# Latent attention with queries on the partitions of the score tile and all keys along its free axis

## The chip, the core and the metric

The kernel runs on one core of a Trainium2 chip. The metric is the device time of one execution in microseconds (us). In the core, TensorE multiplies matrices and writes the results to PSUM, of which the kernel's pools take eight banks of 128 partitions x 512 fp32 numbers; VectorE does elementwise work and reductions along the free axis; ScalarE evaluates functions (exponentials among them) and makes copies; GpSimd and SyncE here issue DMA transfers. Every engine works through its own list of instructions in order and waits for semaphores of the others.

## What is computed

The reference is a two-layer network over 1024 latent tokens and 256 context tokens of width 1024. Layer 0 mixes tokens by multi-head latent attention, layer 1 by long convolutions (computed through block transforms on TensorE). The change is in the attention of layer 0, whose core in the reference is this (the context tokens' keys are set behind the latent tokens' keys, 1280 in all; `ctx_out` plays no part in the output):

```python
def scores(qn_, qr_, kn_, kr_):
    s = jnp.einsum('bqhd,bkhd->bhqk', qn_, kn_) + jnp.einsum('bqhr,bkr->bhqk', qr_, kr_)
    return s.astype(jnp.float32) * scale

def attend(blk):
    qn_b, qr_b = blk
    s = jnp.concatenate([scores(qn_b, qr_b, kn, kr), scores(qn_b, qr_b, knc, krc)], axis=-1)
    p = jax.nn.softmax(s, axis=-1).astype(v.dtype)
    return (jnp.einsum('bhqk,bkhd->bqhd', p[..., :L], v)
            + jnp.einsum('bhqk,bkhd->bqhd', p[..., L:], vc))
...
y = (o * jax.nn.silu(gate)) @ w_out
```

There are 8 heads. A head has 128 plain dimensions and shares 64 rotary dimensions of the key with all heads; values have 128 dimensions. Queries come from a compressed vector of 384, keys and values from one of 256.

## The kernel before

Nearly every product is done with split operands: a float32 matrix is taken apart into a rounded part (hi) and a rest (lo), both of type float32r, and a product is the sum of three matmuls, hi*hi + hi*lo + lo*hi. `mm3` (L117) issues them at L119, L120 and L121, and `split` (L95) makes the parts: ScalarE casts to hi at L96 and VectorE subtracts at L97. All these matmuls, casts and subtractions carry those lines, whatever they are for, so they are told apart by the names of their tiles.

Layer 0's input part leaves the compressed vectors `ckv` (keys and values, 1280 tokens) and `cq` (queries) in SBUF, the rotary keys as `krh` (hi, twice, on the two halves of the partitions) and `krl` (lo, and a 65th row of ones). `attention` (L651 to L850) goes through four pairs of heads (`pr`), two heads of a pair (`j`) and two halves of the queries (`sl`): 16 units of 512 queries of one head.

Ahead of a unit, `ahead` (L746) makes what it needs, through a pool of two PSUM banks "pj": `keys` (1280 keys of one head), `rope` (rotary parts of the queries, for both heads of the pair), `queries`, and then `row_max` (L724 to L739). The exponential needs the maximum of each query's scores, and in the unit's own score tiles the queries lie along the free axis, where a maximum over keys would go across partitions. So `row_max` computes the scores a second time the other way round, queries on the partitions, from the hi parts alone (one matmul at L731 and one at L732 for every 512 keys, in two banks "apx" of their own), takes maxima along the free axis (L733, L735), turns them into a row (L738) and puts that row, negated, into row 64 of the tile `r2` (L739). Together with the row of ones in `krl` it subtracts the maximum within the score matmul at L795.

`attend` (L773) then takes the ten tiles of 128 keys. Each has a score tile S of 128 keys x 512 queries, five matmuls (three of `mm3`, L794 and L795), in one of three banks; ScalarE exponentiates it (L797) into `p`; `split` makes its two parts; VectorE adds `p` to a running sum `acc` (L804); and two tiles later `weigh` multiplies the parts by the values of that tile (`value`, L680) into the bank O. Since keys lie on the partitions of `p`, it is the operand that this product needs as it stands. At the end of a unit the sums over keys are taken on TensorE (L821, a column of ones against `acc`), turned into reciprocals (L823), spread over all partitions (L828), and multiplied in together with the gate, a tile loaded from DRAM (L816, L829); the result goes to DRAM.

The loop at L833 interleaves the tiles of one unit with the tail of the one before it and with two steps of `ahead` for the next. In the last unit `out_first` (L873), the output projection of the first half of the tokens, takes the place of `ahead`. Within these bounds a planner sets the order of the instructions of each engine when the kernel is built, and so TensorE's list mixes matmuls of these pieces. PSUM holds two banks "pj", one O, three S and two "apx": all eight.

Layer 1 matters here for one thing: it turns 128x128 tiles on TensorE (L1033, L1168), with the same call that the change uses.

Of the kernel before, what the change touches and what calls it, by code (L numbers as in the profile page):

```python
# [11 lines left out]
F32 = mybir.dt.float32  # L12
# [7 lines left out]
P = 128  # L20
# [26 lines left out]
def run(gen):  # L47
    """The value that a generator returns."""
    while True:
        try:  # L50
            next(gen)
        except StopIteration as e:
            return e.value


class Net:
# [42 lines left out]
    def feed(self, tiles, bufs=3, side=None):  # L99
        """The weights [128, K * 128] of the coming projections, in their order."""  # L100
# [4 lines left out]
    def weights(self):  # L105
        """The next piece of the weights, the one after it being loaded as well."""
# [26 lines left out]
    def ada(self, layer, part, page, bank, width=1024, queue=None):  # L133
        """part 0: shift and scale, part 1: gate."""
# [66 lines left out]
    def ring(self, two, page, ze, zo, same):  # L201
        """Residues of 8-tile sequences ze (mod x^1024-1), zo (mod x^1024+1) in the 8 blocks."""
# [17 lines left out]
        B = [page().rearrange("p (s j c) -> p s j c", s=2, j=2) for _ in range(2)]  # [+-, j]  # L220
# [3 lines left out]
        t = page().rearrange("p (r s c) -> p r s c", r=2, s=2)  # [re/im, +-]  # L224
# [26 lines left out]
    def forward(self, two, bank, mats, i, b):  # L251
        """Spectrum of block i, [128, (re | im)] in one bank."""
# [92 lines left out]
    def rms(self, xs, n, bank, sqtile):  # L345
        """1/rms of n <= 512 tokens as columns [128, n / 128]."""
# [30 lines left out]
    def spread(self, r, nt, bank):  # L377
        """Columns [128, nt] as a row of nt*128 tokens on every partition."""
# [6 lines left out]
    def modulate(self, x, R, gs, sh, hi, lo):  # L385
        """x is overwritten by x*gs*R; hi + lo = that + shift."""
# [5 lines left out]
    def project(self, srcs, bank):  # L392
        """One M-tile: the next weights against each (hi tiles, lo tiles) of srcs; a bank for each."""
# [15 lines left out]
    def project_first(self, srcs, bank):  # L409
        """The same in the order of srcs; yields before the second of them."""  # L410
# [11 lines left out]
    def layer0_in(self):  # L422
# [13 lines left out]
        self.kr_d = [self.dram.tile([65, NK], F32, name=f"kr_d{r}") for r in range(2)]  # L436
# [39 lines left out]
        def hilo_out(t, n, dsts):  # L476
            """The two parts of t[:n] to DRAM, t being overwritten."""
# [19 lines left out]
        def context():  # L497
            # context: keys and values only
# [19 lines left out]
            hilo_out(ts[2], 64, [d[0:64, new] for d in self.kr_d])  # L518
            yield from normed(ts[:2], "kvg", self.ckv_d, new)
            one = page()  # L520
            v.memset(one[64:65, :], 1.0)
            for o in range(0, NK, LC):
                nc.sync.dma_start(out=self.kr_d[1][64:65, o : o + LC], in_=one[64:65, :LC])

        def latent_kv():
# [10 lines left out]
            for h, sl in enumerate(halves):  # L536
# [6 lines left out]
                hilo_out(t, 64, [d[0:64, sl] for d in self.kr_d])  # L543
            yield

        def latent_q():
# [8 lines left out]
            for h, sl in enumerate(halves):  # L555
                for _ in normed([t[h] for t in ts], "qg", self.att[3], sl, True):
                    next(more, None)
                    yield
# [49 lines left out]
    def attention_loads(self, side, raws):  # L608
# [3 lines left out]
        krh = ap.tile([P, NK], F32R, name="krh")  # L612
        krl = ap.tile([65, NK], F32R, name="krl")
# [5 lines left out]
        self.att = ckv, krh, krl, cq, cos, sin  # L619
# [31 lines left out]
    def attention(self):  # L651
        nc, a = self.nc, self.a
# [5 lines left out]
        ckv, krh, krl, cq, cos, sin = self.att  # L658
        self.og_d = self.dram.tile([HEADS, P, L], F32, name="og_d")
        identr = tp.tile([P, P], F32R, name="identr", bufs=1)  # L660
        act.copy(out=identr, in_=self.ident)
        pick = tp.tile([P, 4, P], F32, name="pick", bufs=1)
        v.memset(pick, 0.0)
        for t in range(4):
# [738 lines left out]
```

## Time and profile before

| | |
|---|---|
| time, median of 3 runs | 1750.57 us (1749.73 to 1758.41) |
| profiled execution: span from the first to the last instruction | 1753.2 us |
| granted TensorE clock, mean over the span | 0.995 |
| attention, from its first key projection to its last products | about 440 to 970 us |

The span is that of one execution under the profiler; the time of an execution also counts what lies around its first and last instruction, and for the profiled one no time is listed beside the span. The two agree within 0.2%.

How the profile is read: PE is a matmul on TensorE, PEld the load of its stationary operand, which overlaps matmuls; DVE is VectorE, ACT ScalarE, POOL GpSimd, SP SyncE. A row names the line of the kernel, the engine and operation, the tiles written and read (out<-in), shapes and types, and the number of instructions (x). Matmuls are pipelined: each has a duration longer than the distance between the starts of two neighbours. "Idle before" is the idle time of an engine right before the instructions of a row, with what ended it (<-). A small matmul of plain fp32 operands shows as two instructions.

### The profile page before, as it was taken

How to read it: one execution, taken by the hardware profiler on the slowest of the kernel's cores; microseconds unless marked ns; L12 is line 12 of the kernel's file. 1: busy time of each engine (PE TensorE's matmuls, PEld its weight loads, DVE VectorE, ACT ScalarE, POOL GpSimd, SP SyncE). 2: the span in 40 equal slices, each digit the busy share in tenths (PEclk: the TensorE clock that was granted, in tenths of full speed). 3: DMA queues.
4: the chain of work that ended last, by engine and by line, in shares of the span. 5: the costliest groups of instructions: out<-in, count | busy, mean ns of one | idle time of the engine just before them, and what ended most of it. 6: DMA issues, size and time to landing. Idle time of an engine off the chain costs nothing.

```text
span 1753.2 us, 23341 instructions
## 1 busy us (share of the span) xinstructions
PE 1687.9 (96%) x8368; PEld 1310.8 (75%) x8368; DVE 1408.3 (80%) x2528; ACT 759.3 (43%) x1315; POOL 15.1 (1%) x43
## 2 busy tenths in 40 slices
PE   7999999799999999999999999999999999999996
PEld 2367666687788888888877766888888888887874
DVE  4786978796687877887877455999999999999956
ACT  4533444435455555555555344433433343343313
POOL 1000000000000000000000010000000000000000
PEclk9999999999999999999999999999999999999999
DMA  9766666436101001010022772232332333234545
GB/s 308 249 186 193 193 199 204 138 93 194 36 27 43 19 29 40 19 32 25 19 67 79 245 249 87 84 101 88 106 114 81 104 87 111 91 118 128 188 149 209
DMA packets 139033, 207.23 MB, mean 118 GB/s; under 512 B 13386, under 2 KB 67361, under 8 KB 138788
## 3 DMA queue, kind: packets, MB, share of 16 engines
q1 hardware_dynamic: 135780, 195.05, 35.6%
q0 software_dynamic: 3136, 10.69, 1.9%
q8 instruction: 66, 1.08, 0.3%
q14 instruction: 51, 0.42, 0.1%
HBM read 149.97 MB, written 53.61 MB: 116 GB/s over the span
## 4 chain that ended last, share of the span: by engine, by line
PE 81%; DMA 9%; DVE 6%; ACT 2%; issue 1%; SPq 1%; DVEq 0%; ACTq 0%
PE pj L119 12%; PE pj L121 12%; PE pj L120 12%; PE apx L731 2%; PE S L119 2%; PE S L795 2%; PE S L120 2%; PE S L794 2%; PE S L121 2%; PE apx L732 2%; PE O L121 2%; PE O L120 2%; PE O L119 2%; PE fu L119 2%; DMA dec<-in_dec 2%; PE fy L119 2%
## 5 line engine op out<-in xcount | busy, mean ns | idle before, releaser
L96 ACT CAST w<-wr 128x512 fp32r<-128x512 f32 (+1 forms) x154 | 93.7, 609 | 276.0 <-PE pj L120 150.3
L119 PE MATMUL pj<-a,w 128*128 128x512 f32 x512 | 203.2, 397 | 1.7 <-ACT a L389 1.7
L120 PE MATMUL pj<-a,w 128*128 128x512 f32 x512 | 203.3, 397 | 0.0
L121 PE MATMUL pj<-a,w 128*128 128x512 f32 x512 | 203.1, 398 | 0.0
L797 ACT ACTIVATE p<-S 128x512 f32<-128x512 f32 x160 | 95.7, 598 | 167.6 <-PE S L795 160.7
L97 DVE TENSOR_TENSOR w<-wr,w 128x512 fp32r<-128x512 f32 (+1 forms) x154 | 102.0, 670 | 63.4 <-ACT w L96 63.0
L804 DVE TENSOR_TENSOR acc<-acc,p 128x512 f32<-128x512 f32 x144 | 99.1, 688 | 29.0 <-ACT p L797 28.6
L97 DVE TENSOR_TENSOR p<-p 128x512 fp32r<-128x512 f32 x160 | 109.7, 685 | 8.9 <-ACT p L96 8.6
L96 ACT CAST bh<-raw 128x512 fp32r<-128x512 f32 x128 | 77.1, 620 | 88.2 <-DVE raw L1043 70.3
L119 PEld LDWEIGHTS pj<-a,w 128*128 128x128 f32 x512 | 96.4, 188 | 22.9 <-ACT a L389 2.4
L120 PEld LDWEIGHTS pj<-a,w 128*128 128x128 f32 x512 | 96.5, 188 | 21.4 <-issue 1.7
L121 PEld LDWEIGHTS pj<-a,w 128*128 128x128 f32 x512 | 96.6, 189 | 18.5 <-DVE w L97 0.3
L733 DVE TENSOR_REDUCE cm<-apx 128x1 f32<-128x512 f32 (+1 forms) x192 | 108.3, 594 | 2.2 <-PE apx L732 1.5
L96 ACT CAST p<-p 128x512 fp32r<-128x512 f32 x160 | 99.4, 621 | 5.0
L121 PE MATMUL pj<-pg,w 128*128 128x512 f32 (+1 forms) x248 | 95.7, 387 | 4.2 <-DVE w L97 4.2
L119 PE MATMUL pj<-pg,w 128*128 128x512 f32 (+1 forms) x248 | 95.7, 387 | 0.6 <-ACT pg L389 0.5
L120 PE MATMUL pj<-pg,w 128*128 128x512 f32 (+1 forms) x248 | 96.3, 388 | 0.0
L97 DVE TENSOR_TENSOR bl<-raw,bh 128x512 fp32r<-128x512 f32 x128 | 84.5, 684 | 9.1 <-ACT bh L96 8.8
L119 PE MATMUL u<-bh,fm 128*128 128x256 f32 (+1 forms) x200 | 66.6, 334 | 11.1 <-ACT bh L96 10.7
L731 PE MATMUL apx<-kn,qn 128*128 128x512 f32 (+1 forms) x192 | 69.9, 369 | 2.9 <-DVE cm L733 2.8
L305 DVE TENSOR_TENSOR kk<-ph,dec 128x512 f32<-128x512 f32 x64 | 42.6, 684 | 32.9 <-DMA dec<-in_dec 20.0
L119 PE MATMUL fy<-bh,dm 128*128 128x256 f32 (+1 forms) x200 | 64.1, 320 | 2.4 <-ACT bh L96 2.4
(297 smaller groups left out, 4396.8 us busy)
## 6 DMA issues: line engine op xcount, KB each, us to landing
aw<-in_adaw SPq DMA_DIRECT2D x32, 512.0 KB, 5.0
kd<-ko SPq DMA_DIRECT2D x128, 128.0 KB, 2.0
wr<-in_hw SPq DMA_DIRECT2D x64, 256.0 KB, 2.6
kt<-kd SPq DMA_DIRECT2D x56, 256.0 KB, 2.7
wr<-in_w SPq DMA_DIRECT2D x34, 256.0 KB, 3.5
dec<-in_dec SPq DMA_DIRECT2D x64, 128.0 KB, 2.5
pg<-in_adaw SPq DMA_DIRECT2D x32, 256.0 KB, 6.1
wr<-in_wo SPq DMA_DIRECT2D x32, 256.0 KB, 3.2
```

Source lines behind the costliest of these rows:

```text
L96: self.nc.scalar.copy(out=hi, in_=raw)
L97: self.nc.vector.tensor_tensor(out=lo, in0=raw, in1=hi, op=ALU.subtract)
L119: mm(out, lhsT=w[0], rhs=x[0], start=start, stop=False)
L120: mm(out, lhsT=w[0], rhs=x[1], start=False, stop=False)
L121: mm(out, lhsT=w[1], rhs=x[0], start=False, stop=stop)
L305: nc.vector.tensor_tensor(out=kk, in0=ps, in1=dec.broadcast_to([P, 2, 2, P]), op=ALU.mult)
L731: mm(b[:, :w], lhsT=qn[0][:, c], rhs=kn[0][:, o : o + w], start=True, stop=False)
L732: mm(b[:, :w], lhsT=r1[:, c], rhs=krh[:, o : o + w], start=False, stop=True)
L733: v.tensor_reduce(out=cm[:, t, i : i + 1], in_=b[:, :w], axis=AX.X, op=ALU.max)
L794: mm(S, lhsT=krh[:, c], rhs=r1, start=False, stop=False)
L797: act.activation(out=p, in_=S, func=AF.Exp, scale=ASCALE)
L804: v.tensor_tensor(out=acc, in0=acc, in1=p, op=ALU.add)
```

## The change

The score tile is set the other way round. A unit is now 256 queries of one head, 32 units in all, each with two row blocks of 128 queries. `scores` computes a row block against all 1280 keys, 128 queries on the partitions and the keys along the free axis, in two and a half PSUM banks, with the same five products (the lo part of the rotary keys now lies in `kr[1]`, without a row of ones). VectorE reduces the whole row block to its maxima, negated, and ScalarE exponentiates it with that column as bias and gives the sums over the row as well. The factor of the softmax is moved into the queries.

Now the queries lie on the partitions of `p`, and the product with the values wants the keys there. So `turn` transposes two key tiles of both row blocks on TensorE (four transposes of 128x128) into a bank and splits them from there, and `weigh` multiplies them by the values, 256 queries at a time. `norm` turns the reciprocals of the sums in the same way and multiplies the gate by them, and O is multiplied by that once. `row_max`, `acc`, the sums on TensorE and the constant tiles `identr` and `pick` are gone, with the row of ones and the five small transfers that wrote it.

PSUM is split anew: five banks for two row blocks of scores (the third is shared by them), one O, and two banks "m" for everything else. The loop issues, for each of five steps of a unit, one `turn`, one or two pieces of the scores of the next units, one `weigh` of the step before, and up to three matmuls' worth (on a running account) of `ahead`. Weights of the next pair are loaded as soon as the keys and queries of this pair are issued. `out_first` begins with the last but one unit and opens its PSUM banks only when its heads are loaded.

The core of the diff, with `attention`'s removed lines left out where they are printed above:

```diff
-        bank = lambda: ps.tile([P, 512], F32, tag="pj", name="pj")
-        px = self.open("psX", 2, space=PSUM)
+        bank = lambda: ps.tile([P, 512], F32, tag="m", name="m")
+        S = self.open("psX", 1, space=PSUM).tile([P, 2 * NK], F32, name="S")
         tp = self.open("attt", 2)
...
+        ssegs = [ksegs, [(256, 512), (768, 512), (0, 256)]]
...
-            self.split(b, qn[0], qn[1])
+            act.activation(out=qn[0], in_=b, func=AF.Copy, scale=ASCALE)
+            v.scalar_tensor_tensor(out=qn[1], in0=b, scalar=ASCALE, in1=qn[0], op0=ALU.mult, op1=ALU.subtract)
...
-        def row_max(kn, qn, r1, r2):
-            cm = tp.tile([P, 4, 3], F32, tag="cm", name="cm")
...
-        units = [(pr, j, sl) for pr in range(HEADS // 2) for j in range(2) for sl in halves]
+        units = [(pr, j, h, q) for pr in range(HEADS // 2) for j in range(2) for h in range(2) for q in range(2)]
...
+            nxt = self.kvw, *self.qw
             for pr in range(HEADS // 2):
+                wc, wq, wr = nxt
                 vals[pr] = (wc, [])
                 rr = {}
                 for j in range(2):
+                    while at["unit"] // 4 < 2 * pr + j - 1:
+                        yield None
+                    kn = [tp.tile([P, NK], F32R, tag=f"kn{r}", name="kn") for r in range(2)]
+                    yield from keys(wc, j, kn)
+                    if j == 1 and pr + 1 < HEADS // 2:
+                        wc = self.load_kv_weights(pr + 1)
+                    for h, sl in enumerate(halves):
+                        while at["unit"] // 2 < 4 * pr + 2 * j + h - 2:
+                            yield None
                         if j == 0:
+                            rr[h] = yield from rope(wr, sl)
                         qn = queries(wq, j, sl)
+                        ready[pr, j, h] = (kn, qn, rr[h][j])
+                        yield 9
+                if pr + 1 < HEADS // 2:
+                    nxt = wc, *self.load_q_weights(pr + 1)
...
+        credit = 0
+        def advance(n):
+            nonlocal credit
+            credit = min(credit + n, n)
+            while credit > 0:
+                cost = next(bg, None)
+                if cost is None:
+                    break
+                credit -= cost
+        def need_values(pr, n):
+            while len(vals[pr][1]) < n:
+                vals[pr][1].append(value(vals[pr][0], len(vals[pr][1])))
+        live = {}
+        def scores(u, s):
+            pr, j, h, q = units[u]
+            at["unit"] = max(at["unit"], u)
+            while (pr, j, h) not in ready:
+                next(bg)
+            kn, qn, r1 = ready[pr, j, h]
+            if s == 0:
+                stat = [tp.tile([P, 2], F32, tag=f"s{i}", name="stat", bufs=4) for i in range(3)]
+                gate = tp.tile([P, 256], F32, tag="gt", name="gt", bufs=3)
+                o = 512 * h + 256 * q
+                nc.sync.dma_start(out=gate, in_=self.gate_d[2 * pr + j, :, o : o + 256])
+                live[u] = {"p": [], "stat": stat, "gate": gate}
+            me = live[u]
+            nm, sm, _ = me["stat"]
+            c = slice(256 * q + P * s, 256 * q + P * s + P)
+            base = NK * s
+            for o, w in ssegs[s]:
+                b, ks = S[:, base + o : base + o + w], slice(o, o + w)
+                mm(b, lhsT=qn[0][:, c], rhs=kn[0][:, ks], start=True, stop=False)
+                mm(b, lhsT=qn[0][:, c], rhs=kn[1][:, ks], start=False, stop=False)
+                mm(b, lhsT=qn[1][:, c], rhs=kn[0][:, ks], start=False, stop=False)
+                mm(b, lhsT=r1[:, c], rhs=kr[0][:, ks], start=False, stop=False)
+                mm(b, lhsT=r1[:, c], rhs=kr[1][:, ks], start=False, stop=True)
+                if (o, w) != ssegs[s][-1]:
+                    yield
+            row = S[:, base : base + NK]
+            v.tensor_reduce(out=nm[:, s : s + 1], in_=row, axis=AX.X, op=ALU.max, negate=True)
+            p = tp.tile([P, NK], F32, tag="p", name="p", bufs=4)
+            act.activation(out=p, in_=row, func=AF.Exp, bias=nm[:, s : s + 1], accum_out=sm[:, s : s + 1])
+            me["p"].append(p)
+        def turn(u, k):
+            me = live[u]
+            b = bank()
+            for i in range(2):
+                t = 2 * k + i
+                for s in range(2):
+                    o = 256 * i + P * s
+                    nc.tensor.transpose(out=b[:, o : o + P], in_=me["p"][s][:, P * t : P * t + P], identity=self.ident)
+            me[k] = [tp.tile([P, 512], F32R, tag=f"p{r}", name="pe", bufs=4) for r in range(2)]
+            self.split(b, *me[k])
+        def norm(u):
+            me = live[u]
+            _, sm, r = me["stat"]
+            v.reciprocal(out=r, in_=sm)
+            b = bank()
+            for s in range(2):
+                nc.tensor.transpose(out=b[:, P * s : P * s + P], in_=r[:, s : s + 1].broadcast_to([P, P]),
+                                    identity=self.ident)
+            g = tp.tile([P, 256], F32, tag="gR", name="gR")
+            v.tensor_tensor(out=g, in0=me["gate"], in1=b[:, 0:256], op=ALU.mult)
+            me["gR"] = g
+        def weigh(u, k):
+            pr, j, h, q = units[u]
+            me = live[u]
+            need_values(pr, 2 * k + 2)
+            if k == 0:
+                me["O"] = ps.tile([P, 512], F32, tag="O", name="O", bufs=1)
+            O = me["O"][:, 0:256]
             hd = slice(P * j, P * j + P)
...
+            pe = me.pop(k)
+            for i in range(2):
+                t = 2 * k + i
                 vv = vals[pr][1][t]
+                sl = slice(256 * i, 256 * i + 256)
+                self.mm3(O, (vv[0][:, hd], vv[1][:, hd]), (pe[0][:, sl], pe[1][:, sl]), t == 0, t == nt - 1)
+            if k == nt // 2 - 1:
+                out = tp.tile([P, 256], F32, tag="og", name="og")
+                v.tensor_tensor(out=out, in0=O, in1=me["gR"], op=ALU.mult)
+                o = 512 * h + 256 * q
+                nc.sync.dma_start(out=self.og_d[2 * pr + j, :, o : o + 256], in_=out)
+                del live[u]
+        def pieces(gen):
+            return lambda: next(gen, None)
+        while (0, 0, 0) not in ready:
+            next(bg)
+        for _ in scores(0, 0):
+            pass
+        need_values(0, 4)
+        for _ in scores(0, 1):
+            pass
+        need_values(0, 8)
+        for _ in scores(1, 0):
+            pass
+        need_values(0, nt)
+        first = None
+        for u in range(nu):
+            sb = pieces(scores(u + 1, 1)) if u + 1 < nu else None
+            sa = pieces(scores(u + 2, 0)) if u + 2 < nu else None
+            plan = [[sb], [sb], [sb, sa], [sa], [sa]]
+            if u == nu - 2:
+                for _ in bg:
+                    pass
+                self.close("attw", "attq")
                 first = self.out_first("right")
+                state = next(first)
+            for k in range(nt // 2):
+                turn(u, k)
+                for s in plan[k]:
+                    if s is not None:
+                        s()
+                pr, q = units[u][0], u % 8
+                if q == 0 and pr > 0:
+                    need_values(pr, min(nt, 4 + 2 * (k + 1)))
+                if q == 7 and pr + 1 < HEADS // 2 and k > 0:
+                    need_values(pr + 1, k)
+                if k > 0:
+                    weigh(u, k - 1)
+                elif u > 0:
+                    weigh(u - 1, nt // 2 - 1)
+                if k == 2:
+                    norm(u)
+                if first is None:
+                    advance(3)
+                elif u == nu - 1 and state is None:
+                    if k == 0:
+                        self.close("psX")
                     next(first, None)
+                elif state is not None:
+                    state = next(first)
+        weigh(nu - 1, nt // 2 - 1)
         self.close("attt")
```

Outside `attention`, `kr_d` and its loads lose the 65th row:

```diff
-        krh = ap.tile([P, NK], F32R, name="krh")
-        krl = ap.tile([65, NK], F32R, name="krl")
+        kr = [ap.tile([P, NK], F32R, name=f"kr{r}") for r in range(2)]
...
-            nc.gpsimd.dma_start(out=krh[64 * r : 64 * r + 64], in_=self.kr_d[0][0:64])
-        nc.gpsimd.dma_start(out=krl, in_=self.kr_d[1])
+            for t, d in zip(kr, self.kr_d):
+                nc.gpsimd.dma_start(out=t[64 * r : 64 * r + 64], in_=d)
```

More of the change, by code (lines that the diff above doesn't have):

```diff
@@ L517, in context @@
             new = slice(L, NK)
-            hilo_out(ts[2], 64, [d[0:64, new] for d in self.kr_d])
+            hilo_out(ts[2], 64, [d[:, new] for d in self.kr_d])
             yield from normed(ts[:2], "kvg", self.ckv_d, new)
[L520 to L523, printed above, removed]
         def latent_kv():
@@ L618, in attention_loads @@
         self.attw = self.open("attw", 1, side=side)
[L619 removed]
+        self.att = ckv, kr, cq, cos, sin
         yield
@@ L764, in ahead @@
-                        ready[pr, j, sl.start] = (kn, qn, r1, r2)
-        bg = ahead()
-        def advance(n, u):
-            for _ in range(n):
-                if u < len(units) and (units[u][0], units[u][1], units[u][2].start) not in ready:
-                    next(bg, None)
-        def attend(u, pr, j, sl):
-            kn, qn, r1, r2 = ready.pop((pr, j, sl.start))
-            h = 2 * pr + j
-            last = j == 1 and sl.start > 0
-            gate = tp.tile([P, 512], F32, tag="gt", name="gt")
-            nc.sync.dma_start(out=gate, in_=self.gate_d[h, :, sl])
-            acc = tp.tile([P, 512], F32, tag="acc", name="acc")
+                        ready[pr, j, h] = (kn, qn, rr[h][j])
@@ L812, in attend @@
-            for t in range(nt - 2, nt):
-                weigh(t)
-            O = st["O"]
-            o = tp.tile([P, 512], F32, tag="og", name="og")
-            v.tensor_tensor(out=o, in0=O, in1=gate, op=ALU.mult)
-            yield
-            b = bank()
-            for t in range(4):
-                c = slice(P * t, P * t + P)
-                mm(b[32 * t : 32 * t + 32, 0:P], lhsT=self.ones, rhs=acc[:, c], start=True, stop=True, tile_position=(0, 32 * t))
-            ri = tp.tile([P, P], F32, tag="ri", name="ri", bufs=1)
@@ L823, in attend @@
-            v.reciprocal(out=ri, in_=b[:, 0:P])
-            yield
-            R = bank()
-            for t in range(4):
-                c = slice(P * t, P * t + P)
-                mm(R[:, c], lhsT=pick[:, t], rhs=ri, start=True, stop=True)
-            v.tensor_tensor(out=o, in0=o, in1=R, op=ALU.mult)
-            nc.sync.dma_start(out=self.og_d[h, :, sl], in_=o)
-        before, first = iter(()), iter(())
-        for u, (pr, j, sl) in enumerate(units):
-            while (pr, j, sl.start) not in ready:
-                next(bg, None)
-            if u == len(units) - 1:
-                self.close("psX", "attw", "attq")
-                first = self.out_first("right")
-            unit = attend(u, pr, j, sl)
-            for t in range(nt):
-                next(unit)
-                next(before, None)
-                if t > 1:
+                sl = slice(256 * i, 256 * i + 256)
```

92 lines of the change are left out of this document (15 added, 77 removed).

## The prediction

> **What bounds the kernel now.** I read the page first, then the table by stage for the stretch in which attention runs, then what TensorE waited for inside that stretch, because the change touches attention alone. The page's first lines:
>
> ```profile
> span 1753.2 us, 23341 instructions
> PE 1687.9 (96%) x8368; PEld 1310.8 (75%) x8368; DVE 1408.3 (80%) x2528; ACT 759.3 (43%) x1315; POOL 15.1 (1%) x43
> ```
>
> The table by stage (start and end; busy time and number of instructions of TensorE, its weight loads, VectorE, ScalarE, GpSimd; clock; DMA share; GB/s): the layer's start, its 495 us of steady state, and the output projection behind it.
>
> ```profile
> 440.00:475.00 35.00, 32.43 (x170) 25.30 (x169) 19.63 (x38) 14.98 (x30) 0.00 (x0) 1.00 0.13 38
> 475.00:970.00 495.00, 492.08 (x2472) 398.97 (x2471) 400.71 (x685) 262.56 (x455) 0.00 (x0) 1.00 0.12 38
> 970.00:1025.00 55.00, 51.56 (x222) 38.10 (x221) 22.22 (x33) 18.67 (x32) 1.74 (x4) 1.00 0.77 247
> ```
>
> And all that TensorE waited for from 475 to 970 (who, for whom, us in total, times, longest):
>
> ```profile
> PE pj L119 <- DVE v L97: 1.4, 3, 0.5
> PE apx L731 <- DVE cm L733: 1.4, 1, 1.4
> ```
>
> The reader is to see that TensorE is idle for 2.9 of 495 us, at full clock, while VectorE has 94 us to spare and DMA is at 0.12. So the time of attention is a sum over matmuls, each at the distance from one start to the next, and faster VectorE or ScalarE work buys nothing by itself. Durations of matmuls overlap, so I take starts, from the order in time (start, us, engine, line, operation). First a 512-wide pace and four transposes between such matmuls, in the second layer, which turns tiles with the same call that the change uses:
>
> ```profile
> 1087.15 0.39 PE L121 MATMUL pj<-a,w 128*128 128x512 f32 x1
> ...
> 1087.85 0.39 PE L121 MATMUL pj<-a,w 128*128 128x512 f32 x1
> 1088.08 0.60 PE L1033 MATMUL tr<-ident,ip 128*128 128x128 f32 x4
> 1088.43 0.48 PE L119 MATMUL pj<-a,w 128*128 128x512 f32 x1
> 1088.75 0.39 PE L120 MATMUL pj<-a,w 128*128 128x512 f32 x1
> ```
>
> From 1087.15 to 1087.85 lie three matmuls: **0.233 us** for 512 columns. The four transposes put off what follows: from 1088.08 to 1088.75 is 0.67 us, less the one matmul in it 0.437 us, **0.109 us each**. Then the 256-wide pace, six matmuls from 709.16 to 709.87, 0.71 us, **0.118 us** each, half of the 512-wide one within 2%:
>
> ```profile
> 709.16 0.28 PE L119 MATMUL pj<-wc,ckv 128*128 128x256 f32 x1
> ...
> 709.87 0.40 PE L119 MATMUL O<-p,v 128*128 128x512 f32 x1
> ```
>
> **What goes from TensorE.** The row-maximum pass (L724 to L739) computes each score tile a second time. Its matmuls come in two kinds, L731 and as many L732; these are the groups of the stretch 450 to 975 (count | busy, mean ns | idle before), with the VectorE reductions that read them:
>
> ```profile
> L731 PE MATMUL apx<-kn,qn 128*128 128x512 f32 x128 | 51.2, 407 | 2.2 <-DVE cm L733 2.1
> L731 PE MATMUL apx<-kn,qn 128*128 128x256 f32 x64 | 18.8, 294 | 0.6 <-DVE cm L733 0.6
> L733 DVE TENSOR_REDUCE cm<-apx 128x1 f32<-128x512 f32 x128 | 85.1, 682 | 2.0 <-PE apx L732 1.5
> L733 DVE TENSOR_REDUCE cm<-apx 128x1 f32<-128x256 f32 x64 | 26.6, 416 | 0.2
> ```
>
> At the paces that is 2 x 128 x 0.233 + 2 x 64 x 0.118 = **74.7 us**. Three small fp32 groups go too, once in each of the 16 units: the maxima turned into a row (L738), the sums over keys (L821), and the reciprocal spread over the partitions (L828).
>
> ```profile
> 492.15 0.40 PE L738 MATMUL pj<-identr,mx 128*1 128x128 f32 x4
> 492.39 0.45 PE L119 MATMUL pj<-ckv,wc 128*128 128x512 f32 x1
> 492.67 0.39 PE L120 MATMUL pj<-ckv,wc 128*128 128x512 f32 x1
> 498.73 0.39 PE L119 MATMUL S<-qn,kn 128*128 128x512 f32 x1
> 499.05 0.42 PE L821 MATMUL pj<-acc,ones 128*32 128x128 f32 x8
> 499.40 0.50 PE L120 MATMUL S<-qn,kn 128*128 128x512 f32 x1
> 499.75 0.40 PE L121 MATMUL S<-qn,kn 128*128 128x512 f32 x1
> 503.22 1.06 PE L828 MATMUL pj<-ri,pick 128*128 128x128 f32 x8
> 504.06 0.49 PE L731 MATMUL apx<-kn,qn 128*128 128x512 f32 x1
> 504.40 0.39 PE L732 MATMUL apx<-krh,r 128*128 128x512 f32 x1
> ```
>
> By the same reading: L738 0.52 - 0.233 = 0.287, L821 1.02 - 2 x 0.233 = 0.554, L828 1.18 - 0.233 = 0.947, together 1.79 us, x 16 = **28.6 us**. Removed: 74.7 + 28.6 = **103.3 us**.
>
> **What comes to TensorE.** There are 32 units of 256 queries. Each turns 2 row blocks x 10 key tiles, five groups of four: 160 x 0.437 = **69.9 us**. Each has one group of two for the reciprocals: 2 x 0.109 x 32 = **7.0 us**. The products with the values become 960 matmuls of 256 columns in place of 480 of 512: 113.3 for 111.8, **+1.5 us**. The scores have the same columns with the roles swapped: 640 x 0.233 + 320 x 0.118 = 186.9 for 800 x 0.233 = 186.4, **+0.5 us**. Projections of keys, values, queries and rotary parts are the same matmuls. Added: **78.9 us**. TensorE's work falls by 103.3 - 78.9 = **24.4 us**.
>
> One rule of the Trainium skill speaks against this. TensorE: Matmul & The Clock Gate, Part 4: PE-mode transpose, gives about 275 ns for a 128x128 transpose in a kernel's context and says that the full clock does not engage for it; by that figure the 704 transposes would cost some 194 us (an estimate from that page) and the change would lose. The row above disagrees for the pace: four in 0.437 us, at clock 1.00. The case without overlap stands among the rivals at a price of its own.
>
> **What the other engines do.** They must stay hidden. In the stretch 450 to 975:
>
> ```profile
> L804 DVE TENSOR_TENSOR acc<-acc,p 128x512 f32<-128x512 f32 x144 | 99.1, 688 | 29.0 <-ACT p L797 28.6
> L97 DVE TENSOR_TENSOR p<-p 128x512 fp32r<-128x512 f32 x160 | 109.7, 685 | 8.9 <-ACT p L96 8.6
> L797 ACT ACTIVATE p<-S 128x512 f32<-128x512 f32 x160 | 95.7, 598 | 167.6 <-PE S L795 160.7 <-DVE acc L804 5.2 <-PE S L120 1.1
> L96 ACT CAST v<-pj 128x256 fp32r<-128x256 f32 x40 | 14.5, 366 | 6.1 <-PE pj L121 5.6
> L96 ACT CAST kn<-pj 128x512 fp32r<-128x512 f32 x14 | 8.2, 587 | 13.2 <-PE pj L121 13.1
> ```
>
> VectorE's running sum (L804) goes, 99 us, for ScalarE sums as it exponentiates. The 192 reductions, 112 us, become 64 of 1280 columns: (682 - 416) / 256 = 1.04 ns a column, so 682 + 768 x 1.04 = 1.48 us, 95 us in all. The split of the exponentials stays, 160 times, now read from PSUM. VectorE ends some 115 us lighter. One exponential takes 1280 columns: ScalarE's slope is (587 - 366) / 256 = 0.86 ns, so 598 + 768 x 0.86 = 1.26 us, and with a bias column and the sum I take 1.4, within 1.26 to 1.6; 64 of them are 90 us for 95.7 before. Neither engine comes near TensorE. The wider key tiles, gates in 32 loads of half the size, and the weights' earlier loads are costed at nothing: DMA at 0.12 covers them. If one came late, it would show once for each of four head pairs, under 1 us each.
>
> **The waits that come.** Each of the 64 row blocks now runs in series: last score matmul, 1.48 us of reduction, 1.4 us of exponential, with the score region held until then. Behind the exponential on ScalarE wait the casts that empty the two banks "m" through which turns, keys, values, queries and reciprocals all pass; on VectorE the splits wait behind the reduction. I laid out one unit by hand in the code's order. After a block's last score matmul, the next turn's cast can start about 3 us later and its split ends 1.3 us after that; TensorE meanwhile has two steps of 0.44 + 1.17 + 0.71 = 2.3 us (a turn, five score matmuls, six products) before the product that needs it, and a score region's next fill comes two steps after its drain began. So both waits just fit. One place does not: the reciprocals' turn (`norm`) stands behind a reduction on VectorE, about 0.6 us of TensorE in each of 32 units, 19 us, if the order of the code is kept. It need not be. In the run before, TensorE's order is a planner's: the row-maximum matmuls were set between the score matmuls of one tile. Between 0 and 19 I take the nearer end and a third, **+6 us**. Below nothing: 2.9 us of waits in steady state and 2.6 idle at the start (35 - 32.43) could go, so the bound is -5.
>
> The sum: -24.4 + 6 = **-18 us**. The profiled span, 1753.2, lies 2.6 us above the median of the runs, 1750.57, which also counts what lies outside the first and last instruction; outside attention nothing is edited, so the difference is applied to the median: **1732 us**.
>
> **The rivals.**
>
> *The waits eat the gain* (within 0.5%, 8.8 us, about what a measurement of this kernel can tell from no change): the two banks are used some 280 times (160 turns, 32 reciprocals, 40 values, 24 keys, 16 queries, 8 rotary parts), twice as often as now, and the gain is gone at 24.4 / 64 = 0.38 us of wait for each row block. For it: everything passes a bank that needs both other engines to come free. Against it: they have more room than now, and now TensorE waits 2.9 us. Time about 1749.
>
> *Slower, by the same chain*: if at each row block one more split (0.685) gets between score and exponential, TensorE waits 0.7 us x 64 = 45 us: +20, **1771 us**. It decides above 0.5 us for each block.
>
> *The transposes do not overlap*: each then costs its recorded duration,
>
> ```profile
> L1033 PE MATMUL tr<-ident,ip x128: 270/272/303, 1086.5 to 1555.8; 128*128 128x128 f32 x128
> ```
>
> 0.272 for 0.109 us, 704 x 0.163 = +115, about 1847 us. Against it speak the four starts within 0.35 us above. (That is what the skill's page would make of it.)
>
> *The score regions wait for each other*, because both lie in one PSUM tile: each fill would then stand behind the other's drain, 64 x 2.9 us, and the time would be over 1900. Against it: in the second layer a transpose that reads one part of a tile starts while VectorE still writes other parts.
>
> ```profile
> 1227.41 2.49 DVE L1046 SCALAR_TENSOR_TENSOR z<-rg,z 128x512 f32<-128x512 f32 x4
> 1228.21 0.14 PEld L1168 LDWEIGHTS tr<-ident,z 128*128 128x128 f32 x1 [0.23 <-issue]
> ```
>
> **How the numbers follow.** Forecast, a gain of more than 8.8 us: 0.60, likeliest 1732, its own range 1718 (24.4 + 5 and a little) to 1742. Waits eat it: 0.20. Slower by the chain: 0.15. Transposes: 0.03. Regions: 0.02. So faster 0.60, same 0.20, slower 0.20. The range runs from 1718 to 1772: below it I leave 0.06, above it the two dear rivals and the worst of the chain, 0.12.
>
> **What would show it.** Right: starts 0.11 us apart inside a group of four transposes; paces of 0.118 and 0.233; VectorE's busy time in attention under 300 us; TensorE's waits in steady state under 10 us in all, and most of them before the reciprocals' turn. Wrong: TensorE waiting for casts of "m" (two banks), for the exponential (regions), or for a split of a turned tile (the chain); a granted clock below 1.00 in attention; or reductions far over 1.5 us.

## The result and the profile after

The changed kernel takes **1773.19 us** (median of 4 runs, 1769.72 to 1775.65) where the kernel before takes 1751.03 (4 runs): ratio 1.0103, 95% interval 1.0069 to 1.0137. It is slower by 22 us; 18 us of gain were forecast. The profiled execution took 1773.0 us at a span of 1771.2.

The table by stage of the changed kernel, as it was read before the change (start and end, length; busy time and instructions of TensorE, its weight loads, VectorE, ScalarE, GpSimd; clock; DMA share; GB/s):

```profile
440.00:475.00 35.00, 30.94 (x172) 25.35 (x173) 18.00 (x29) 15.59 (x29) 0.00 (x0) 1.00 0.09 25
475.00:970.00 495.00, 477.86 (x3014) 414.87 (x3013) 281.41 (x426) 220.31 (x383) 0.00 (x0) 1.00 0.12 35
```

TensorE now idles for 17.1 of the 495 us, against 2.9, while VectorE fell from 401 to 281 busy us and the clock stayed at 1.00. What TensorE waited for in that stretch (who, for whom, us in total, times, longest):

```profile
PE m L805 <- DVE pe L97: 5.4, 12, 0.7
PE S L784 <- ACT p L794: 3.2, 4, 1.0
PE m L119 <- DVE pe L97: 2.1, 3, 0.7
PE O L120 <- DVE pe L97: 2.0, 4, 0.6
PE m L805 <- DVE kn L97: 1.6, 6, 0.3
```

Recorded durations of matmuls overlap, so idle time understates a wait. I therefore took all matmuls of attention, from the first key projection to the last product, in the kernel before and in the changed one,

```profile
440.33 0.39 PE L119 MATMUL pj<-ckv,wc 128*128 128x512 f32 x1
...
966.57 0.39 PE L121 MATMUL O<-p,v 128*128 128x512 f32 x1
```

```profile
437.11 0.39 PE L119 MATMUL m<-ckv,wc 128*128 128x512 f32 x1
...
985.68 0.28 PE L121 MATMUL O<-pe,v 128*128 128x256 f32 x1
```

and subtracted from each distance between two starts its pace (0.232, 0.119 and, for a group of four transposes, 0.438 us: the prediction's within 1%; the three small groups of the kernel before at the prediction's prices). What is left is called **late** below.

| attention | us in all | at the paces | late |
|---|---|---|---|
| before | 526.2 | 516.2 | 10.0 |
| after | 548.6 | 498.3 | 50.2 |

The stretch after holds 12 more matmuls of the output projection (60 for 48, 2.8 us), and the last unit's sums and reciprocals lie behind the stretch before (1.5 us). Like for like, TensorE's work fell by 17.9 + 2.8 + 1.5 = 22.2 us, where the sum had 24.4, and 40.2 us of waiting came. Together that is +18.0 us, and the spans of the two profiled executions differ by 18.0. Of the 50.2, 16 lie ahead of turns (L805), 13 ahead of scores (L784, L785), 10 ahead of products (O), most of the rest ahead of projections: no single row of the waits says what the cause is. The order in time does. One half unit near the end of attention, with the exponential before it (start, us, engine, line, operation):

```profile
950.37 1.34 ACT L794 ACTIVATE p<-S,stat 128x1280 f32<-128x1280 f32 x1
...
951.95 0.40 PE L784 MATMUL S<-kn,qn 128*128 128x512 f32 x1
...
954.72 0.28 PE L788 MATMUL S<-kr,r 128*128 128x256 f32 x1
...
955.04 1.49 DVE L792 TENSOR_REDUCE stat<-S 128x1 f32<-128x1280 f32 x1 [2.05 <-PE S L788]
...
956.57 1.33 ACT L794 ACTIVATE p<-S,stat 128x1280 f32<-128x1280 f32 x1 [0.45 <-DVE stat L792]
957.04 0.41 DVE L838 TENSOR_TENSOR og<-O,gR 128x256 f32<-128x256 f32 x1
957.18 0.66 PE L805 MATMUL m<-ident,p 128*128 128x128 f32 x4 [0.59 <-DVE pe L97]
...
957.79 0.19 ACT L794 ACTIVATION_READ_ACCUMULATOR p<-S,stat 128x1 f32 x1
957.80 0.28 PE L120 MATMUL O<-pe,v 128*128 128x256 f32 x1
957.88 1.07 ACT L96 CAST pe<-m 128x512 fp32r<-128x512 f32 x2
957.92 0.28 PE L121 MATMUL O<-pe,v 128*128 128x256 f32 x1
958.04 0.50 PE L784 MATMUL S<-kn,qn 128*128 128x512 f32 x1
```

The row block's 15 score matmuls run here in one unbroken bunch, 951.95 to 954.84; the reduction and the exponential follow; and the next bunch, of the *other* row block, starts at 958.04, just behind the exponential's end, although its own region had been free since the exponential of 950.37, for 6 us. Counted over the whole trace, of 960 score matmuls **none** starts between the start of a row block's reduction and the end of its exponential. Only 13 of the 64 blocks run unbroken; the others have turns and products between their pieces. But each of the 63 blocks after the first begins 0.14 to 0.31 us after the end of the other region's exponential. While a block is drained, some 3 us, TensorE has turns, products and projections alone; they come faster than the two banks "m" are emptied and wait for the splits. By this reading the rows in the list of waits are consequences, and the first experiment tests it.

The durations were as forecast: the reduction 1485 ns (forecast 1.48 us), the exponential 1331 ns with 195 more to read out its sum (forecast 1.4, within 1.26 to 1.6), 64 of each:

```profile
L792 DVE TENSOR_REDUCE stat<-S 128x1 f32<-128x1280 f32 x64 | 95.0, 1485 | 43.6 <-PE S L788 43.6
L794 ACT ACTIVATE p<-S,stat 128x1280 f32<-128x1280 f32 x64 | 85.2, 1331 | 42.6 <-DVE stat L792 41.8
L794 ACT ACTIVATION_READ_ACCUMULATOR p<-S,stat 128x1 f32 x64 | 12.5, 195 | 0.0
```

### The profile page after: what moved, and what is told of

It reads as the page before. It is cut to its first block, busy times and chain, and to the rows that moved or that the text cites. A ratio compares the mean times of both kernels' runs of the same rounds, so it can differ in the third digit from the quotient of the medians.

```text
span 1771.2 us, 24402 instructions
## 1 busy us (share of the span) xinstructions
PE 1691.4 (95%) x9008; PEld 1344.4 (76%) x9008; DVE 1293.1 (73%) x2266; ACT 722.9 (41%) x1250; POOL 17.0 (1%) x44
## 4 chain that ended last, share of the span: by engine, by line
PE 78%; DMA 8%; DVE 7%; ACT 3%; issue 2%; SPq 1%; DVEq 0%; ACTq 0%
PE pj L119 11%; PE pj L120 11%; PE pj L121 11%; PE m L805 3%; PE S L784 2%; PE m L119 2%; PE S L785 2%; PE S L787 2%; PE S L786 2%; PE S L788 2%; PE m L120 2%; PE m L121 2%; PE ad L147 2%; PE fu L119 2%; PE fy L119 2%
## 5 line engine op out<-in xcount | busy, mean ns | idle before, releaser
L96 ACT CAST w<-wr 128x512 fp32r<-128x512 f32 (+1 forms) x154 | 93.5, 610 | 276.4 <-PE pj L120 156.9
L97 DVE TENSOR_TENSOR pe<-m,pe 128x512 fp32r<-128x512 f32 x160 | 108.4, 686 | 62.4 <-ACT pe L96 62.3
L96 ACT CAST pe<-m 128x512 fp32r<-128x512 f32 x160 | 92.0, 587 | 119.4 <-PE m L805 117.9
L792 DVE TENSOR_REDUCE stat<-S 128x1 f32<-128x1280 f32 x64 | 95.0, 1485 | 43.6 <-PE S L788 43.6
L805 PE MATMUL m<-ident,p 128*128 128x128 f32 x640 | 98.5, 276 | 8.0 <-DVE pe L97 5.4
L794 ACT ACTIVATE p<-S,stat 128x1280 f32<-128x1280 f32 x64 | 85.2, 1331 | 42.6 <-DVE stat L792 41.8
L119 PE MATMUL O<-pe,v 128*128 128x256 f32 x320 | 97.7, 305 | 0.8 <-ACT pe L96 0.2
L120 PE MATMUL O<-pe,v 128*128 128x256 f32 x320 | 92.4, 289 | 3.2 <-DVE pe L97 2.8
L121 PE MATMUL O<-pe,v 128*128 128x256 f32 x320 | 90.2, 282 | 0.0
L805 PEld LDWEIGHTS m<-ident,p 128*128 128x128 f32 x640 | 73.6, 140 | 21.0 <-DVE pe L97 9.1
```

Of the source, the lines that this page charges most:

```text
L96: self.nc.scalar.copy(out=hi, in_=raw)
L97: self.nc.vector.tensor_tensor(out=lo, in0=raw, in1=hi, op=ALU.subtract)
L119: mm(out, lhsT=w[0], rhs=x[0], start=start, stop=False)
L120: mm(out, lhsT=w[0], rhs=x[1], start=False, stop=False)
L121: mm(out, lhsT=w[1], rhs=x[0], start=False, stop=stop)
L792: v.tensor_reduce(out=nm[:, s : s + 1], in_=row, axis=AX.X, op=ALU.max, negate=True)
```

## The experiments

Theory A: the two score regions wait for each other because they are parts of one PSUM tile. Rival B: two banks "m" are too few, or VectorE's splits stand behind its reductions. Rival C came later: the planner's order of the instructions is itself the loss.

### Regions free of each other

The edit takes the order between a score matmul and the other row block's reduction and exponential away, but for the last piece, which lies in the one bank that both regions share:

```diff
+        drains = [[], []]
 ...
-                mm(b, lhsT=qn[0][:, c], rhs=kn[0][:, ks], start=True, stop=False)
+                ms = [mm(b, lhsT=qn[0][:, c], rhs=kn[0][:, ks], start=True, stop=False),
 ...
                 if (o, w) != ssegs[s][-1]:
+                    for m in ms:
+                        for other in drains[1 - s][-2:]:
+                            self.tc.declare_no_dep(m.ins, other.ins, reason="other banks")
                     yield
 ...
+            drains[s] += [red, ex]
```

> The changed kernel, with the first two pieces of each row block's scores (in PSUM banks of their own) no longer ordered behind the other row block's reduction and exponential; the last piece, which lies in the bank that both blocks share, keeps that wait. Theory A (the two score regions wait for each other, because they lie in one PSUM tile): most of the some 50 us by which TensorE's matmuls come later than their paces in attention go, 15 to 20 stay; 1735 to 1748 us, below the kernel before (1751). Rival B (the two banks "m" are too few for 280 uses, or VectorE's splits stand behind its reductions): the late matmuls stay, 1765 us or more.

Measured: **1726.72 us** (4 runs) beside 1753.06 for the kernel before, ratio 0.9842, interval 0.9812 to 0.9873. The same work, 46 us less than the changed kernel. The steady stretch of this run, in which the list of TensorE's waits is empty:

```profile
475.00:935.00 460.00, 459.80 (x3049) 416.45 (x3048) 289.49 (x435) 226.17 (x388) 0.00 (x0) 1.00 0.14 41
```

Attention takes 503.3 us, 498.3 at the paces and 5.0 late. And 307 score matmuls now start within the other block's reduction and exponential. In the order in time (line numbers are five or fewer higher here; L785 begins a piece, L798 is the exponential):

```profile
904.95 0.40 PE L785 MATMUL S<-kn,qn 128*128 128x512 f32 x1
...
905.84 1.48 DVE L796 TENSOR_REDUCE stat<-S 128x1 f32<-128x1280 f32 x1
905.88 0.39 PE L789 MATMUL S<-kr,r 128*128 128x512 f32 x1
...
907.35 1.33 ACT L798 ACTIVATE p<-S,stat 128x1280 f32<-128x1280 f32 x1 [2.15 <-DVE stat L796]
907.39 0.47 PE L785 MATMUL S<-kn,qn 128*128 128x512 f32 x1
907.71 0.39 PE L786 MATMUL S<-kn,qn 128*128 128x512 f32 x1
```

One piece stands beside the reduction, the next beside the exponential, with a turn and products between. Theory A holds, with more than it promised (5 late for the 15 to 20 it left, and a time below its 1735 to 1748); rival B, which wanted 1765 or more, falls. With the order between the regions gone, the planner also set TensorE's instructions in another order, so this run alone does not tell waits from order. This version also beats the kernel before, by 26 us.

### The exponential twice, with the regions ordered and free

If the exponential stands in a chain that everything waits for, lengthening it must cost in the changed kernel and not with the regions free. The edit, in both:

```diff
+            act.activation(out=p, in_=row, func=AF.Exp, bias=nm[:, s : s + 1])
             act.activation(out=p, in_=row, func=AF.Exp, bias=nm[:, s : s + 1], accum_out=sm[:, s : s + 1])
```

> The changed kernel with a second exponential of each row block (without the sum, its result overwritten), 1.33 us of ScalarE more in each of 64 chains. Theory A: chain of a block from the first score matmul to the end of the exponential grows from 6.5 us to 7.9 and blocks stand one behind the other, so 64 x 7.9 = 506 us is a floor for a stretch in which TensorE also has to do work that finds no room beside it: +45 to +85 us, 1818 to 1858. Rival B: ScalarE has room (240 of 549 us busy), and only casts that happen to stand behind the added instruction come later: under +25 us.

> Both edits together: regions free of each other and the exponential twice. Theory A: with the regions apart a block's chain has two half units (about 15 us) for its 7.9 us, so the second exponential costs little here: within 25 us of the run with free regions alone. Rival B: the added exponential costs as much here as it does with the regions ordered, whatever that is.

Measured (a single run each): 1813.28 us in the changed kernel, **+40.1**; 1731.39 with the regions free, **+4.7**. The first is 5 us below theory A's span, the second within it; rival B wanted under 25 us in the first and the same cost in both. The kernel before, run beside each batch of experiments, took 1753 to 1759 us (medians), so times of single runs compare to some 5 us; the lateness of attention, read from the traces, compares better. It is 93.5 and 12.6 us, where it is 50.2 and 5.0 without the second exponential: +43.3 and +7.6. So 64 x 1.33 = 85 us of added ScalarE work cost half of their length in the one kernel and almost nothing in the other: the exponential was in TensorE's way by the order alone.

### The tile or the shared bank

The regions share one bank, and a wait over that bank could look like a wait over the tile. Two runs give each region three banks of its own, once as parts of one tile and once as two tiles; the sixth bank comes from "m":

```diff
-        bank = lambda: ps.tile([P, 512], F32, tag="m", name="m")
-        S = self.open("psX", 1, space=PSUM).tile([P, 2 * NK], F32, name="S")
+        bank = lambda: ps.tile([P, 512], F32, tag="m", name="m", bufs=1)
+        S = self.open("psX", 1, space=PSUM).tile([P, 3072], F32, name="S")
 ...
-        ssegs = [ksegs, [(256, 512), (768, 512), (0, 256)]]
+        ssegs = [ksegs, ksegs]
 ...
-            base = NK * s
+            base = 1536 * s
```

```diff
+        px = self.open("psX", 1, space=PSUM)
+        S = [px.tile([P, 1536], F32, name=f"S{i}") for i in range(2)]
 ...
+            base = 0
 ...
-                b, ks = S[:, base + o : base + o + w], slice(o, o + w)
+                b, ks = S[s][:, base + o : base + o + w], slice(o, o + w)
```

> The changed kernel with the score tile widened from five PSUM banks to six, so that each row block has three banks of its own and none is shared; the sixth comes from the tiles named m, which have one bank here in place of two. Beside it runs the same with two score tiles of three banks each. Theory A1 (the fills are ordered because both regions are parts of one tile, whichever banks they lie in): this run is 20 to 50 us longer than the one with two tiles. Theory A2 (they are ordered because of the shared bank): both are within 10 us of each other. Rival B's price by itself: one bank m has to be filled, cast (0.59 us) and split (0.69) some 280 times in 500 us, so both runs should stand well above the run with free regions, by 30 us or more.

> Two score tiles of three banks each, one bank for the tiles named m. Theory A1: 20 to 50 us shorter than the run with one tile of six banks; A2: within 10 us of it. Against the run with free regions in five banks (1727 us) it shows what the second bank m is worth: by rival B much, 30 us or more; if theory A is all there is, some 10 to 30.

Measured (a single run each): 1956.92 and 1930.08 us, 27 apart, within what A1 asked. The times alone would be weak, since one bank "m" drowns both; the order is not. With one tile of six banks, again **none** of 960 score matmuls starts between the start of the other block's reduction and the end of its exponential, though no bank is shared; with two tiles 549 do, and nothing else was edited. Here one block's exponential at 807.92 has the other block's fill beside it:

```profile
807.60 0.80 PE L785 MATMUL S<-kn,qn 128*128 128x512 f32 x1 [0.23 <-ACT p L795]
807.92 1.34 ACT L795 ACTIVATE p<-S,stat 128x1280 f32<-128x1280 f32 x1
808.19 0.63 PE L786 MATMUL S<-kn,qn 128*128 128x512 f32 x1
808.62 0.60 PE L787 MATMUL S<-kn,qn 128*128 128x512 f32 x1
```

The one tile is the cause. The Trainium skill (Perfetto Trace Analysis, Optimizing Tensor Performance, Matmuls) says that independent groups of matmuls should rotate through different PSUM banks, so that emptying one overlaps the next group. By these two runs different banks are not enough: parts of one tile took turns as if they were one bank.

The runs also price rival B. Two tiles with one bank "m" take 203 us more than free regions with two. I had expected some 10 to 30 if theory A were all there is, and 30 or more by B. So the banks do matter, from two down to one (about 40 us of it passed while the granted clock was at 0.50); at two, with the regions free, 5.0 us late in all is what they can cost.

### The order of the code in place of the planner's

Both kernels with TensorE's instructions of attention kept in the order in which the code issues them:

```diff
+        with self.tc.manual_schedule(engines={mybir.EngineType.PE}):
 ...
             for u in range(nu):
```

> The changed kernel with TensorE's instructions of attention kept in the order in which the code issues them, in place of the planner's. Theory A: in that order the second block's last piece and the first block's next first piece stand side by side (third step of each unit), and the latter waits there for a whole reduction and exponential, 3 us, and at the unit's first step about 1 us more: 32 x 4 = 130 us above the run with free regions, about 1850; the planner's bunches were its way around the wait. If the planner's order were itself the loss (rival C), this run would come below 1773.

> Order of the code and regions free of each other. This is what the prediction laid out by hand: waits of 0 to 19 us, 19 if each of the 32 turns of the reciprocals stands 0.6 us behind a reduction. Theory A: 1727 to 1746 us. If the order of the code alone costs much more than that, the layout by hand in the prediction was wrong too.

Measured (a single run each, in one order of TensorE's instructions): **2016.58** us with the regions ordered, **1742.92** with them free. Rival C falls, since the code's order is worse by 243 us; it was the planner's order that kept the loss at 46. And TensorE's list is the same in the two runs, matmul for matmul, all 3284 of attention: the waits between the regions, with the slow clock behind them, cost 274 us there. The expectation of 1850 was far too low, by two terms. From 475 to 1200 us TensorE waited 60 times, 3.0 us each, at both fills of a unit:

```profile
PE S L784 <- ACT p L794: 181.5, 60, 5.3
```

and behind many of the waits it runs slowly for a while:

```profile
917.43 0.61 PE L784 MATMUL S<-kn,qn 128*128 128x512 f32 x1 [2.56 <-ACT p L794]
917.84 0.63 PE L785 MATMUL S<-kn,qn 128*128 128x512 f32 x1
918.27 0.63 PE L786 MATMUL S<-kn,qn 128*128 128x512 f32 x1
...
921.62 0.40 PE L785 MATMUL S<-kn,qn 128*128 128x512 f32 x1
921.86 0.39 PE L786 MATMUL S<-kn,qn 128*128 128x512 f32 x1
```

0.43 us from start to start after the wait, 0.23 again 4 us later. The granted clock (the last number but two) shows the same:

```profile
917.66:921.08 3.42, 3.42 (x13) 2.93 (x13) 0.01 (x1) 0.00 (x0) 0.00 (x0) 0.50 0.00 0
921.08:924.45 3.37, 3.37 (x24) 2.95 (x22) 1.10 (x2) 1.08 (x2) 0.00 (x0) 1.00 0.12 39
```

The steady stretch in the table by stage has a granted clock of 0.88, where the changed kernel had 1.00:

```profile
475.00:970.00 495.00, 375.71 (x2050) 329.12 (x2050) 198.15 (x291) 153.40 (x259) 0.00 (x0) 0.88 0.07 20
```

Of attention's 295 us late, 206 lie at waits, as starts show them (the list, by idle time, has 181.5 for the 60), and 84 at matmuls that ran while the granted clock was at 0.50, 195 us in all.

The second run is what the prediction had laid out by hand: 16 us above the planner's order by the times, 14.6 by lateness (19.6 for 5.0), within the 0 to 19 it gave. The place it named for them, the reciprocals' turn, is not where they lie. Of the waits from 440 to 960 us the largest is for the rotary parts of the queries, and only a fraction stands behind `norm`'s multiplication (gR):

```profile
PE S L788 <- DVE r L710: 5.0, 2, 3.6
...
PE m L119 <- DVE gR L824: 1.5, 3, 0.5
```

### The turns issued twice

With the regions free, each transpose of the turns a second time over the first:

```diff
                     nc.tensor.transpose(out=b[:, o : o + P], in_=me["p"][s][:, P * t : P * t + P], identity=self.ident)
+                    nc.tensor.transpose(out=b[:, o : o + P], in_=me["p"][s][:, P * t : P * t + P], identity=self.ident)
```

> Free regions, and each of the 640 transposes of the turns issued twice, the second over the first. It measures the term of the sum that the prediction took from the second layer (0.109 us each) and that the Trainium skill prices higher (TensorE: Matmul & The Clock Gate, Part 4: PE-mode transpose, about 275 ns). If TensorE's sum of paces sets the time and 0.109 us is right: 640 x 0.109 = 70 us above the run with free regions, 1797, give or take 8. If transposes do not overlap (0.272): +174, about 1901. If the waits set the time and TensorE has slack: under +35.

Measured (a single run): 1794.88 us, +68.2, that is 68.2 / 640 = **0.107 us** for a transpose; attention in the trace is longer by 69.8 us (573.1 for 503.3), 0.109 each. Eight in a row, between products and scores:

```profile
700.18 0.28 PE L810 MATMUL m<-ident,p 128*128 128x128 f32 x1
700.29 0.27 PE L811 MATMUL m<-ident,p 128*128 128x128 f32 x1
700.40 0.27 PE L810 MATMUL m<-ident,p 128*128 128x128 f32 x1
...
700.95 0.27 PE L811 MATMUL m<-ident,p 128*128 128x128 f32 x1
```

Recorded at 0.27 us, they start 0.11 apart: the duration overlaps, the price is the pace. The Trainium skill's 275 ns (TensorE: Matmul & The Clock Gate, Part 4: PE-mode transpose) is the duration of the row; as a price it would be two and a half times what this run measured.

### The reciprocals applied by GpSimd

A try at 7 us more: the rows of the exponentials are multiplied by their reciprocals on GpSimd, and `norm` goes.

```diff
+            r = me["stat"][2]
+            v.reciprocal(out=r[:, s : s + 1], in_=sm[:, s : s + 1])
+            nc.gpsimd.tensor_scalar(out=p, in0=p, scalar1=r[:, s : s + 1], scalar2=None, op0=ALU.mult)
 ...
-                if k == 2:
-                    norm(u)
```

> Free regions, and the reciprocals applied to the rows of the exponentials by GpSimd (128 x 1280 times a column, 64 times) in place of being turned and spread on TensorE: 64 transposes, 32 uses of a bank m, 32 multiplications of VectorE go. By the paces 7.0 us of TensorE's work go: 1720 us, if GpSimd's pass (not shown by any trace so far) is done within the two steps, 4.6 us, that a row block has between its last score matmul and its turn beyond reduction and exponential (3.0 us), so under some 1.6 us. If it takes longer, or slows VectorE beside it, the turns wait: 1727 to 1770.

Measured: 1779.4 us, ratio to the kernel before 1.0137, interval 1.0108 to 1.0166: 53 us worse than free regions alone, and 9 above the upper end of what I expected. GpSimd's pass takes 3.53 us, twice the slack of 1.6, and the turns wait for it (65 us late, 42 of them ahead of turns). It also holds up VectorE beside it, as the last section shows. The group, and the first row of TensorE's waits from 440 to 960 us:

```profile
L802 POOL TENSOR_SCALAR p<-p,stat 128x1280 f32<-128x1280 f32 x64 | 225.9, 3530 | 336.5 <-DVE stat L801 311.0 <-PE O L121 17.8 <-PE m L813 7.7
```

```profile
PE m L813 <- POOL p L802: 17.9, 10, 2.2
```

## Why the prediction was wrong

- **What bounds the kernel**: right. TensorE's sum of paces set the time before, and sets it again once the regions are free.
- **TensorE's work, -24.4 us**: right within some 2 us, -22.2 at the paces. The difference lies in the third decimal of the paces (0.119 for 0.118, 0.232 for 0.233), times some 1000 matmuls each. The transposes' price (0.109) was measured at 0.107 to 0.109 by doubling them; the rival that follows from the Trainium skill's rule (TensorE: Matmul & The Clock Gate, Part 4: PE-mode transpose), at 0.03, did not come true.
- **What the other engines do**: right. Reduction and exponential fell where they were put, and VectorE's busy time over attention went from 417 to 307 us, 110 less (forecast 115).
- **The waits, +6 us**: this term failed, +40 (from 10.0 to 50.2 us late). The step in it is the sentence that a region's "next fill comes two steps after its drain began". It let a region wait for its own drain alone. In the changed kernel each fill waits for the drain of the other region too, so there is one region in effect, and scores, reduction and exponential stand in a row. With that order gone the layout holds: late falls to 5.0 us, 5 less than in the kernel before, which is the bound of -5 that the prediction gave for this term, and 1726.7 us lies 5 below the forecast of 1732.
- **The rival that was the cause**, "the score regions wait for each other", was on the list at 0.02. It was rejected on a row in which a transpose reads one part of the tile z while VectorE writes others. That row was about another thing: a tile in SBUF and a reader, not one in PSUM and a writer behind a reader. It could not carry the rejection, and I had found no row of a PSUM tile with two regions filled and drained in turn.
- **That rival's price**, 64 x 2.9 us and over 1900, was right for the order of the code (60 x 3.0 us, and 2016 with the slow clock). In the planner's order most of each drain is covered by turns, products and projections, and some 45 us remain (50.2 late for 5.0). A rival was thus thrown out with a price that did not belong to the order that the planner built.
- **Slower by the same chain**, 1771 us, is near the measured time by chance: its mechanism, a split between score and exponential, would have stayed with the regions free.
- **The bounds**: 1773.19 lies just above the upper end of 1772.
- **What would show it**: paces, clock 1.00 and durations came as said; VectorE's busy time, to be under 300 us, was 307. TensorE's listed waits passed the 10 us, and the largest rows are waits for splits, which the prediction had named as the sign of the chain; "for the exponential (regions)" has 3.2 us only. The signs thus pointed at the wrong rival first, and the size of the wait showed in starts, not in idle time.

What stays open: how the 45 us divide between waits at run time and the order that the planner set because of them. In the code's order TensorE's list is the same in both runs, and only the waits differ. Open too is the rule by which the parts of one PSUM tile take turns; the runs show that they do, in banks of their own as well.

## What to carry to other kernels

A buffer that two pieces of work use in turn has to be two buffers for whatever orders the work, not only two halves with banks of their own: ask of each wait which *other* reader it also waits for, and look for a write that starts while the other half is being read. A rival that a row seems to exclude is excluded only if the row shows the same memory, the same pair of accesses and the same order. When TensorE is late at many places by a little each, sum the starts against the paces before reading the list of waits; the rows in it may all be consequences.

## What the runs showed of the hardware

- In the code's order with the regions ordered, the granted clock fell to 0.50 for 3.4 or 6.8 us at a time, and 512 columns took 0.43 us in place of 0.23. From 475 to 1235 us, each of the 30 waits of 3.7 us or more had such a stretch, from within the wait or at most 2 us behind it; so had 14 of the 23 waits of 2.0 to 2.7 us, and none of the six of 1.6. Attention was 295 us late for 181.5 us of listed waits, 1.6 times as much. The Trainium skill (TensorE: Matmul & The Clock Gate, Part 1, HAM oscillation) puts the limit at gaps of more than about 3.4 us; here 2.56 us were enough in the rows above, and not every time. In the changed kernel, with no wait over 1.0 us in the list above, the clock stayed at 1.00.
- The sum of an exponential is a second instruction of 0.195 us on ScalarE.
- Beside a GpSimd pass (3.53 us), VectorE's instructions that read PSUM kept their time: the split of 512 columns took 0.69 us within it. Instructions of 512 columns with both operands in SBUF that began within a pass ended 0.1 us behind the pass, all 17 of them, and took up to 3.4 us for the 0.69 that the same ones take with no pass beside them. So the length goes by when the pass ends, not by a factor. One pass, with an instruction of each kind in it (two subtractions stand in the last row, the second behind the pass):

```profile
568.45 3.52 POOL L802 TENSOR_SCALAR p<-p,stat 128x1280 f32<-128x1280 f32 x1 [4.84 <-DVE stat L801]
568.67 0.69 DVE L97 TENSOR_TENSOR pe<-m,pe 128x512 fp32r<-128x512 f32 x1 [0.31 <-ACT pe L96]
569.39 3.39 DVE L710 TENSOR_TENSOR r<-rp,r 64x512 fp32r<-64x512 f32 x2
```
